# Where the sums of the modulation groups stand in a two-layer trunk kernel, and the order of its last norm

## The chip, the cores and the metric

The kernel runs on one core of a Trainium2 chip. The metric is the device time of one execution in microseconds (us). Before the change it is 2019.62 us, the median of 3 runs (2019.18 to 2021.65).

The core has a matrix engine (TensorE, PE, with its weight loads listed as PEld), a vector engine (VectorE, DVE), a scalar engine (ScalarE, ACT), GpSimd (POOL) and SyncE (SP), whose queue issues most DMA transfers. Each engine works through its own instructions in order.

## The reference

A trunk of two layers (T = 512 tokens, D = 1024, float32). Each layer has a mixer sub-layer and a feed-forward (FFN) sub-layer, and both are modulated by a vector c (adaLN):

```
m = silu(c) @ w_ada + b_ada          # six groups of 1024 values for each layer
h = rms_norm(x) * gain * (1 + scale) + shift          # groups 0 and 1 (mixer), 3 and 4 (FFN)
z = h @ w_in                          # inputs of three branches, and three gates
y_a = head_rms(scan_a(...)) * sigmoid(a_g)            # gated recurrence, both directions
y_b = head_group_norm(scan_b(...)) * silu(b_g)        # retention, both directions
y_c = head_rms(scan_c(...)) * silu(c_g)               # gated linear attention, both directions
mixed = sum over branches of sigmoid(gate) * (y @ w_p)
x = x + m[2] * (mixed @ w_out)                        # group 2
x = x + m[5] * ((silu(g) * u) @ w_ffn_out)            # g, u = h @ w_ffn_in; group 5
```

After the last layer comes a final RMS norm with a gain, which is the output.

## The kernel before

**Matrix products.** Every float32 product is three products of halves: an operand is split into a high part and the rest, and `three` (L278) adds hi·hi, lo·hi and hi·lo. Weights come in tiles of 128 x 4 x 256 (512 KB). `weight` (L259) takes a buffer `raw` (a pool of 3) and loads it on SP's queue; `parts` (L268) splits a part of the tile, high part by ACT (L274), rest by DVE (L275), into buffers of which there are four each. A tile has two splits, and its `raw` buffer is free once both are done. Names of tiles carry the layer, the matrix and the place: `L0fg6w40l` is layer 0's FFN matrix g, column block 6, rows from 4 on, half 0, the rest (l) of the split (h is the high part).

**The order of the work.** A scheduler sorts each engine's instructions by its own estimate of when they are due. `tc.high_priority` moves some ahead, `tc.issue_after` holds an instruction behind another in the schedule, and `in_order` (L103) ties a piece of the program to the order in which it is written. The boundary between two sub-layers is written with `in_order`; the last norm is not.

**The stages of a layer.** Input products and three branches with their scans; a tail of the mixer (the C branch's last levels `L0CQ`, `L0CK`, `L0Ct`, the gates `ga`, `gb`, `gc`, the products `mpa`, `mpb`, `mpc` and the gate products `mga`, `mgb`, `mgc`); `wo` (w_out); a boundary (`fz`, `fy`, `fx`: rest of w_out, norm, first products of the FFN); `fg` and `fu` (w_ffn_in); `fo` (w_ffn_out); the next boundary.

**Modulation groups.** Groups 0 and 1 of layer 0 are computed at the start, beside the first products. The other ten are background work: each is 16 pieces `wr` of 128 x 512 (256 KB, a pool of 2 buffers, loaded on SP's queue in program order, L204), and each piece is summed against `cact` (silu of c) by one DVE instruction (L210); the last piece of a group also finishes it (L214, L215). `bg_step` (L235) issues the load of the next piece and the sum of the piece loaded the step before. `weight` calls it `k.rate` times behind a tile's load, as long as the group is within `k.ahead`: twice a tile in the mixer's tail and w_out (`RATE`, L54, set at L1149), once a tile in the FFN (L1197). `bg_until` (L246) forces what is left of a group ahead of the place that needs it: group 2 before w_out, group 4 before the FFN's boundary, group 5 before `fo`, and the next layer's group 1 before its boundary.

**The start.** `first_products` (L533) works in eight rounds, one for each 128 rows of x. A round on DVE has two splits of weights, two small instructions, `x0t` (L600), the lower part of `h` (L603), which needs its high part from ACT (L602), and two sums `dot` (L565) for the next round.

**The end.** `last_norm` (L1061) makes the last products in two halves of the tokens, sums the squares (`finacc`), and for each half turns them into a factor for each token (PE `fin0tp`, DVE `fin0r`, POOL, DVE `fin0dg`, PE `fin0bc`), then makes eight outputs (L1078) and stores four of them with each transfer.

Of the kernel before, what the change touches and what calls it, by code (L numbers as in the profile page):

```python
# [50 lines left out]
LATE = (1, 1, 2)  # L51
LAG = 1
LAG1 = 1
RATE = 2  # L54

LEAF = (0, 1, 2, 4, 8, 16)

# [14 lines left out]
class Filler:  # L72
# [43 lines left out]
def trunk_kernel(ctx: ExitStack, tc: tile.TileContext, a, out):  # L116
# [11 lines left out]
    def duo(name, dt=F32, shape=(P, 2, 2, 512)):  # L128
        return sp.tile(list(shape), dt, tag="s", name=name)
# [14 lines left out]
    def xt(kk):  # L144
        return k.xd[kk // 4][:, kk % 4]
# [86 lines left out]
                st.enter_context(tc.issue_after(i.ins))  # L232
            yield

    def bg_step(upto=(DEPTH, 0)):  # L235
        if bg and bg[0][0] <= upto:
            _, (load, step) = bg.pop(0)
            with behind():
                if not k.loaded:
                    load()  # L240
                if bg:
                    bg[0][1][0]()
                k.loaded = True
                step()
# [14 lines left out]
    def weight(src, kn, cols, name):  # L259

        raw = wp.tile([P, 4, 256], F32, tag="raw", name=name)
        nc.sync.dma_start(raw[:, :kn, :cols], src.rearrange("(k p) n -> p k n", p=P))  # L262
        if k.ahead:
            for i in range(k.rate):
                bg_step(k.ahead)
        return raw

    def parts(raw, name):  # L268

        shape = list(raw.shape)  # L270
        hi = wp.tile(shape, F32R, tag="hi", name=name + "h", bufs=4)
        lo = wp.tile(shape, F32R, tag="lo", name=name + "l", bufs=4)
        with behind(), tc.high_priority(offset=k.prio):
            nc.scalar.copy(hi, raw)  # L274
            nc.vector.tensor_sub(lo, raw, hi.bitcast(F32))  # L275
# [257 lines left out]
    def first_products():  # L533
# [57 lines left out]
        def before(kk):  # L591

            hl = [parts(loads[kk][1][:, :3, i * P:(i + 1) * P], f"L0A0w{kk}{i}") for i in range(2)]
            m = mod[0][:, 0:2, kk]
            nc.vector.tensor_add(m, m, acol[:, 0:16].rearrange("p (g k) -> p g k", g=2)[:, :, kk])
            gm = gmul[0][:, 0, kk:kk + 1]
            nc.vector.scalar_tensor_tensor(gm, mod[0][:, 1, kk:kk + 1], 1.0, acol[:, R_N1 + kk:R_N1 + kk + 1],
                                           op0=ALU.add, op1=ALU.mult)
            t, sh = tmp(f"x0t{kk}"), mod[0][:, 0, kk:kk + 1]
            nc.vector.scalar_tensor_tensor(t, xt(kk), gm, bc, op0=ALU.mult, op1=ALU.mult)  # L600
            hi, lo = h[0][kk // 2][:, kk % 2], h[1][kk // 2][:, kk % 2]
            nc.scalar.activation(hi, t, AF.Identity, bias=sh)  # L602
            nc.vector.scalar_tensor_tensor(lo, t, sh, hi.bitcast(F32), op0=ALU.add, op1=ALU.subtract)  # L603
# [456 lines left out]

    def last_norm(block, add):  # L1061
        acc = squares("fin")
        for n in range(4):
            block(0, n)
        norm = half_norm(acc, 0, add, "fin0")
        for _ in range(7):
            bcs = [next(norm)]
        for n in range(4):
            block(1, n)
        norm = half_norm(acc, 1, add, "fin1")  # L1070
        with tc.high_priority(offset=EVAC):
            for _ in range(7):
                bc = next(norm)
        for hv, bc in enumerate(bcs + [bc]):
            od = duo(f"out{hv}", shape=(P, KD, T // 2))
            for kk in range(KD):
                gf = pcol[:, R_NF + kk:R_NF + kk + 1]
                nc.vector.scalar_tensor_tensor(od[:, kk], xt(kk)[:, half(hv)], gf, bc, op0=ALU.mult, op1=ALU.mult)  # L1078
                if kk % 4 == 3:
                    dst = out[(kk - 3) * P:(kk + 1) * P, half(hv)].rearrange("(j p) t -> p j t", p=P)  # L1080
                    nc.sync.dma_start(dst, od[:, kk - 3:kk + 1])


    for l in range(DEPTH):
# [44 lines left out]
        with tc.tile_pool(name=f"att{l}", bufs=2) as k.att:  # L1129
            halves = lambda t: [t[:, 0], t[:, 1]]  # L1130
            y = {"A": halves(claimed(f"L{l}Ay"))}
            lev, tail_a = run(branch_a(l, 0, z0), PACE[0])
            run(lev(), PACE[0])
            done_a = gain_done(l, "A", R_NA, y["A"])
            tail_b = both(branch_b(l, fill.get("zb")), tail_a(va, done_a), PACE[1])
            y["B"] = halves(claimed(f"L{l}By"))
            tail_b = tail_b(fill.get("vb"), gain_done(l, "B", R_NB, y["B"], True))
            lev, tail_a1 = both(branch_a(l, 1, fill.get("z1")), tail_b, PACE[2], 1)
            both(lev(), tail_b, PACE[2])
            lev, tail_c = both(branch_c(l, fill.get("zc")), tail_a1(va, done_a), PACE[3])  # L1140
# [12 lines left out]
        with tc.tile_pool(name=f"late{l}", bufs=1) as k.late:
# [35 lines left out]
            for n in range(KF // 2):  # L1189
                bk = gemmT(w, n * 256, 256, h, f"L{l}fg{n}") if n else first[0]  # L1190
                sg = []
                for i in range(2):
                    s = wk.tile([P, 512], F32, tag="t", name=f"L{l}fs{n}{i}", bufs=5)
                    nc.scalar.activation(s, bk[i], AF.Silu)
                    sg.append(s)
                bk = gemmT(w, DFF + n * 256, 256, h, f"L{l}fu{n}") if n else first[1]
                k.ahead, k.rate, k.prio = (l + 1, 1), 1, AHEAD  # L1197
                for i in range(2):
                    nc.vector.tensor_mul(sg[i], sg[i], bk[i])  # L1199
                    split(hd, 2 * n + i, sg[i])  # L1200
                if n:
                    k.behind = ()
# [74 lines left out]
```

## Time and profile before

| | us |
|---|---|
| median of 3 runs | 2019.62 (2019.18 to 2021.65) |
| profiled execution, its own time | 2018.08 |
| its span | 2016.3 |
| PE busy | 1926.5 (96%) |
| DVE busy | 1076.3 (53%) |
| ACT busy | 763.1 (38%) |
| POOL busy | 172.4 (9%) |
| DVE's sums of pieces (L210) | 111.6, 160 of them |
| DVE waiting for their transfers | 283.4, in 104 places |

The page's mean clock of PE is given as a share of full speed; it is 0.986 over the execution. A row of the waits names the waiting engine, its instruction and line, what ended the wait, and then the time in all, how often, and the longest. A row of a timeline has its start, its duration, engine, line and operation, what is written from what, and in brackets how long the engine stood idle before it and for what. A row of the table by stretches gives the stretch and its length, the busy time of each engine with its number of instructions, PE's granted clock, the busy share of the DMA engines, and GB/s. Idle time of an engine that is not the bound costs nothing by itself.

### The profile page before, as it was taken

To read this page: it belongs to the slowest core of one execution; us is meant where nothing else is said; L and a number is where in the kernel's file an instruction comes from. 1 tells how busy PE (TensorE), PEld (TensorE's weight loads), DVE (VectorE), ACT (ScalarE), POOL (GpSimd) and SP (SyncE) were. 2 spreads that over 40 slices of the span, in tenths; PEclk is the share of its full clock that TensorE was granted. 3 is DMA by queue.
4 is the path that set the end of the run, shared out by engine and by line. 5 is a ranking of instruction groups with operands and counts; after the bars stand their busy time and mean duration, and the time that the engine had idled before them with its cause. 6 is when DMAs were issued, how large, how long until landed. Compare 5 with 4: busy or idle time off the path is not lost. (4 is left out here: it accounts for less than half of the span.)

```text
span 2016.3 us, 32132 instructions
## 1 busy us (share of the span) xinstructions
PE 1926.5 (96%) x13288; PEld 1606.2 (80%) x13288; DVE 1076.3 (53%) x1917; ACT 763.1 (38%) x1273; POOL 172.4 (9%) x175
## 2 busy tenths in 40 slices
PE   5999999899999999999999999999999999999997
PEld 4898877777788887778889988777778888888886
DVE  6676586664436544443355756786553464433334
ACT  3544375432334332222345343653323353333321
POOL 0120111020111000000011101110111110000000
PEclk9999999999999999999999999999899999999998
DMA  9332223444323343433333322334543233333332
GB/s 337 94 106 77 64 77 90 150 149 151 115 94 110 120 141 126 141 125 126 115 120 91 106 76 57 94 97 125 167 156 96 94 121 126 115 95 94 99 94 69
DMA packets 196579, 231.91 MB, mean 115 GB/s; under 512 B 10640, under 2 KB 170640, under 8 KB 195408
## 3 DMA queue, kind: packets, MB, share of 16 engines
q1 hardware_dynamic: 194640, 224.77, 35.5%
q0 software_dynamic: 1504, 4.47, 0.8%
q8 instruction: 104, 1.70, 0.3%
q10 hardware_dynamic: 288, 0.61, 0.1%
q14 instruction: 43, 0.35, 0.1%
HBM read 221.43 MB, written 6.29 MB: 113 GB/s over the span
## 5 line engine op out<-in xcount | busy, mean ns | idle before, releaser
L210 DVE SCALAR_TENSOR_TENSOR wr<-wr,cact 128x512 f32<-128x512 f32 x160 | 111.6, 704 | 283.7 <-DMA wr<-w_ada 283.4
L334 ACT CAST L0hid<-L0fs 128x512 fp32r<-128x512 f32 x22 | 13.6, 621 | 84.5 <-DVE L0fs L1199 84.4
L348 POOL TENSOR_TENSOR L1h0r<-L1h0r,mhalf 128x2 f32<-128x2 f32 x1 | 1.1, 1082 | 358.2 <-DVE L1h0r L347 358.2
L348 POOL TENSOR_TENSOR fin0r<-fin0r,mhalf 128x2 f32<-128x2 f32 x1 | 0.7, 700 | 346.2 <-DVE fin0r L347 346.2
L565 DVE SCALAR_TENSOR_TENSOR fw<-fw,cact 128x1024 f32<-128x1024 f32 x16 | 19.0, 1219 | 0.0
L334 ACT CAST L1hid<-L1fs 128x512 fp32r<-128x512 f32 x22 | 13.7, 623 | 12.3 <-DVE L1fs L1199 11.4
L602 ACT ACTIVATE h<-x0t,mod 128x512 fp32r<-128x512 f32 x8 | 5.8, 722 | 31.9 <-DVE x0t L600 31.8
L1175 POOL TENSOR_TENSOR L0ma<-L0ma,L0sgb 128x512 f32<-128x512 f32 x6 | 9.8, 1638 | 90.6 <-DVE L0sgb L1174 90.6
L1175 POOL TENSOR_TENSOR L1ma<-L1ma,L1sgb 128x512 f32<-128x512 f32 x6 | 9.8, 1638 | 90.4 <-DVE L1sgb L1174 90.4
L1175 POOL TENSOR_TENSOR L1ma<-L1ma,L1sgc 128x512 f32<-128x512 f32 x8 | 12.7, 1599 | 52.0 <-DVE L1sgc L1174 52.0
L1175 POOL TENSOR_TENSOR L0ma<-L0ma,L0sgc 128x512 f32<-128x512 f32 x8 | 12.8, 1599 | 51.1 <-DVE L0sgc L1174 51.1
L577 PE MATMUL ssp<-ones,x0acc 128*128 128x1 f32 x8 | 1.9, 354 | 15.0 <-DVE x0acc L574 15.0
L335 DVE TENSOR_TENSOR L0hid<-L0fs,L0hid 128x512 fp32r<-128x512 f32 x22 | 15.1, 692 | 1.9
L335 DVE TENSOR_TENSOR L1hid<-L1fs,L1hid 128x512 fp32r<-128x512 f32 x22 | 15.2, 693 | 0.8
L686 DVE TENSOR_TENSOR L0AK<-L0AK,L0AG 128x1024 f32<-128x1024 f32 x12 | 14.6, 1216 | 0.7 <-POOL L0AG L678 0.7
L686 DVE TENSOR_TENSOR L1AK<-L1AK,L1AG 128x1024 f32<-128x1024 f32 x12 | 14.6, 1215 | 0.7 <-POOL L1AG L678 0.7
L678 POOL TENSOR_TENSOR L0AqT<-L0AG 128x1024 f32<-128x1024 f32 x2 | 8.0, 4018 | 78.6 <-DVE L0AG L868 78.6
L684 DVE TENSOR_TENSOR L0AQ<-L0AQ,L0AG 128x1024 f32<-128x1024 f32 x12 | 14.6, 1214 | 0.0
L684 DVE TENSOR_TENSOR L1AQ<-L1AQ,L1AG 128x1024 f32<-128x1024 f32 x12 | 14.6, 1213 | 0.0
L577 PEld LDWEIGHTS ssp<-ones,x0acc 128*128 128x128 f32 x8 | 1.8, 327 | 15.0 <-DVE x0acc L574 15.0
L210 DVE DVE_READ_ACCUMULATOR wr<-wr,cact 128x1 f32 x160 | 13.1, 82 | 0.0
L1032 ACT ACT_TABLE_LOAD x10 | 12.8, 1283 | 0.2
(5602 smaller groups left out, 6827.4 us busy)
## 6 DMA issues: line engine op xcount, KB each, us to landing
wr<-w_ada SPq DMA_DIRECT2D x160, 256.0 KB, 4.1
fw<-w_ada SPq DMA_DIRECT2D x16, 512.0 KB, 9.8
L0A0w<-w_in SPq DMA_DIRECT2D x8, 384.0 KB, 8.8
L0fo0w<-w_ffn_out SPq DMA_DIRECT2D x5, 512.0 KB, 3.5
L0fo1w<-w_ffn_out SPq DMA_DIRECT2D x5, 512.0 KB, 3.6
L0fo2w<-w_ffn_out SPq DMA_DIRECT2D x5, 512.0 KB, 3.4
L1hzw<-w_ffn_out SPq DMA_DIRECT2D x5, 512.0 KB, 3.4
L1fo0w<-w_ffn_out SPq DMA_DIRECT2D x5, 512.0 KB, 3.5
```

The source lines that it names most:

```text
L210: nc.vector.scalar_tensor_tensor(t, t, 1.0, cact[:, hlf * 512:hlf * 512 + 512], op0=ALU.mult, op1=ALU.mult, accum_out=st["sum"][:, hlf, j: ...
L334: nc.scalar.copy(h, src)
L335: return nc.vector.tensor_sub(dst[1][i // 2][:, i % 2], src, h.bitcast(F32))
L348: nc.gpsimd.tensor_tensor(r, r, mhalf[:, :w], op=ALU.pow)
L565: nc.vector.scalar_tensor_tensor(t, t, 1.0, cact, op0=ALU.mult, op1=ALU.mult, accum_out=mod[0][:, g, kk:kk + 1])
L577: nc.tensor.matmul(ps[:, c:c + 1], acc[:, c * P:(c + 1) * P], ones[:, :1], start=True, stop=True)
L602: nc.scalar.activation(hi, t, AF.Identity, bias=sh)
L678: nc.gpsimd.tensor_mul(tots[2 * s], t[:, :, :, 0], t[:, :, :, 1])
L684: nc.vector.tensor_mul(q, q, crossed(t, s, 1, d - 1, True))
L686: nc.vector.tensor_mul(kk, kk, crossed(t, s, d + 1, -d - 1, True))
L1032: nc.scalar.activation(z[:, i], z[:, i], func)
L1175: nc.gpsimd.tensor_add(acc[i], acc[i], sg[i])
```

## The change

- `bg_step` is parted. `bg_load` issues the load of one piece, at most two being begun; `bg_sum` issues a sum. `weight` calls `bg_load` once for each tile, in the mixer's tail too (`RATE` is gone), and notes in `k.due` how many sums are due. `parts` issues such a sum behind its own DVE split (`issue_after` on that instruction).
- In the mixer `k.ahead` is set earlier, ahead of the C branch's tail. In the FFN it reaches to group 2 of the next layer, one group further than before.
- In `first_products` one of the two `dot` sums stands between ACT's high part and DVE's lower part of `h`.
- `last_norm` is written in order, its outputs are spread over it, and a store takes two outputs in place of four.

```diff
@@
+    def bg_load(upto=(DEPTH, 0)):
+        if bg and bg[0][0] <= upto and len(k.begun) < 2:
+            tag, (load, step) = bg.pop(0)
             with behind():
+                load()
+            k.begun.append((tag, step))
+    def bg_sum(after=None):
+        with behind():
+            if after is None:
+                k.begun.pop(0)[1]()
+            else:
+                with tc.issue_after(after.ins):
+                    k.begun.pop(0)[1]()
     def bg_until(l, g):
-        while any(tag <= (l, g) for tag, _ in bg):
-            bg_step()
+        while any(tag <= (l, g) for tag, _ in k.begun + bg):
+            bg_load()
+            if len(k.begun) == 2 or not bg:
+                bg_sum()
+        k.due = 0
@@ weight
         if k.ahead:
-            for i in range(k.rate):
-                bg_step(k.ahead)
+            k.due = len(k.begun)
+            bg_load(k.ahead)
@@ parts
-            nc.vector.tensor_sub(lo, raw, hi.bitcast(F32))
+            last = nc.vector.tensor_sub(lo, raw, hi.bitcast(F32))
+        if k.due:
+            k.due -= 1
+            bg_sum(last)
@@ first_products
             nc.scalar.activation(hi, t, AF.Identity, bias=sh)
+            if kk + 1 < KD:
+                dot(kk + 1, 1)
             nc.vector.scalar_tensor_tensor(lo, t, sh, hi.bitcast(F32), op0=ALU.add, op1=ALU.subtract)
             if kk + 1 < KD:
-                dot(kk + 1, 1)
                 dot(kk + 1, 0)
@@ last_norm
-        for n in range(4):
-            block(0, n)
...
+        with in_order(tc):
+            for n in range(4):
+                block(0, n)
+            norm = half_norm(acc, 0, add, "fin0")
+            for _ in range(3):
+                next(norm)
+            block(1, 0)
+            block(1, 1)
+            for _ in range(3):
+                next(norm)
+            block(1, 2)
+            bcs.append(next(norm))
+            block(1, 3)
+            outputs(0, 0, 2)
+            norm = half_norm(acc, 1, add, "fin1")
+            for _ in range(5):
+                next(norm)
+            outputs(0, 2, 4)
+            next(norm)
+            bcs.append(next(norm))
+            outputs(0, 4, 8)
+            outputs(1, 0, 8)
@@ the layers
+            k.ahead = (l, 4)
             run(tail_c(fill.get("vc"), gain_done(l, "C", R_NC, y["C"])), PACE[5])
-        k.ahead, k.rate = (l, 4), RATE
...
-                k.ahead, k.rate, k.prio = (l + 1, 1), 1, AHEAD
+                k.ahead, k.prio = (l + 1, 2), AHEAD
```

How it moves instructions is shown at three places. First, DVE in the tail of layer 0's mixer, around the last level of the C branch; `wr` rows are the sums of pieces (group, block, half). Before:

```order
L275 TENSOR_TENSOR L0mpa0w00l<-L0mpa0w_4305,L0mpa0w00h 128x512
L214 TENSOR_TENSOR mod_93<-ms_2_4068 128x8
L215 TENSOR_TENSOR mod_93<-mod_93,cols 128x8
L275 TENSOR_TENSOR L0mpa0w01l<-L0mpa0w_4305,L0mpa0w01h 128x512
L275 TENSOR_TENSOR L0mpb0w00l<-L0mpb0w_4353,L0mpb0w00h 128x512
L210 SCALAR_TENSOR_TENSOR wr_3_0_1_4443,ms_3_4445<-wr_3_0_1_4443,cact 128x512
L684 TENSOR_TENSOR L0CQ<-L0CQ,L0CG 128x2x8x64
L686 TENSOR_TENSOR L0CK<-L0CK,L0CG 128x2x8x64
L210 SCALAR_TENSOR_TENSOR wr_3_1_0_4447,ms_3_4445<-wr_3_1_0_4447,cact 128x512
L275 TENSOR_TENSOR L0mpb0w01l<-L0mpb0w_4353,L0mpb0w01h 128x512
L210 SCALAR_TENSOR_TENSOR wr_3_1_1_4490,ms_3_4445<-wr_3_1_1_4490,cact 128x512
L210 SCALAR_TENSOR_TENSOR wr_3_2_0_4493,ms_3_4445<-wr_3_2_0_4493,cact 128x512
```

The same place with the change:

```order
L283 TENSOR_TENSOR L0mpa0w00l<-L0mpa0w_4296,L0mpa0w00h 128x512
L209 SCALAR_TENSOR_TENSOR wr_2_3_1_4230,ms_2_3877<-wr_2_3_1_4230,cact 128x512
L283 TENSOR_TENSOR L0mpa0w01l<-L0mpa0w_4296,L0mpa0w01h 128x512
L283 TENSOR_TENSOR L0mpb0w00l<-L0mpb0w_4341,L0mpb0w00h 128x512
L209 SCALAR_TENSOR_TENSOR wr_2_4_0_4298,ms_2_3877<-wr_2_4_0_4298,cact 128x512
L696 TENSOR_TENSOR L0CQ<-L0CQ,L0CG 128x2x8x64
L698 TENSOR_TENSOR L0CK<-L0CK,L0CG 128x2x8x64
L283 TENSOR_TENSOR L0mpb0w01l<-L0mpb0w_4341,L0mpb0w01h 128x512
L283 TENSOR_TENSOR L0mgc0w00l<-L0mgc0w_4384,L0mgc0w00h 128x512
L209 SCALAR_TENSOR_TENSOR wr_2_4_1_4343,ms_2_3877<-wr_2_4_1_4343,cact 128x512
```

There is one sum for each weight tile in place of two, each right behind the tile's first split, and the pieces are at group 2 where they were at group 3 before.

Second, SP's queue in layer 0's FFN, the loads (`fg`, `fu`: weight tiles) around column block 6. Before:

```order
L262 DMA L0fg6w_7132<-w_ffn_in 128x4x256
L204 DMA wr_0_2_1_7134<-w_ada 128x512
L262 DMA L0fg6w_7169<-w_ffn_in 128x4x256
L204 DMA wr_0_3_0_7171<-w_ada 128x512
L262 DMA L0fu6w_7212<-w_ffn_in 128x4x256
L204 DMA wr_0_3_1_7214<-w_ada 128x512
```

With the change:

```order
L269 DMA L0fg6w_7132<-w_ffn_in 128x4x256
L203 DMA wr_0_2_0_7089<-w_ada 128x512
L269 DMA L0fg6w_7169<-w_ffn_in 128x4x256
L203 DMA wr_0_2_1_7134<-w_ada 128x512
L269 DMA L0fu6w_7212<-w_ffn_in 128x4x256
L203 DMA wr_0_3_0_7171<-w_ada 128x512
```

On DVE, the sum behind the first split of the first fg6 tile is that of wr_0_3_1 before (its load stands behind fu6's tile, two tiles further on) and that of wr_0_2_0 with the change (its load stands behind the fg6 tile itself).

Third, DVE at the end of layer 0's w_out, with the change; before, no sum stands here:

```order
L283 TENSOR_TENSOR L0wo2w00l<-L0wo2w_5796,L0wo2w00h 128x512
L209 SCALAR_TENSOR_TENSOR wr_4_5_1_5757,ms_4_5354<-wr_4_5_1_5757,cact 128x512
L283 TENSOR_TENSOR L0wo2w01l<-L0wo2w_5796,L0wo2w01h 128x512
L209 SCALAR_TENSOR_TENSOR wr_4_6_1_5835,ms_4_5354<-wr_4_6_1_5835,cact 128x512
L1210 SCALAR_TENSOR_TENSOR L0x_4885<-L0wo1b_5716,mod_93,L0x_4885 128x512
L283 TENSOR_TENSOR L0wo2w40l<-L0wo2w_5833,L0wo2w40h 128x512
L209 SCALAR_TENSOR_TENSOR wr_4_6_0_5798,ms_4_5354<-wr_4_6_0_5798,cact 128x512
L414 TENSOR_TENSOR L0facc<-L0facc,L0fsq_5889 128x512
L209 SCALAR_TENSOR_TENSOR wr_4_7_0_5872,ms_4_5354<-wr_4_7_0_5872,cact 128x512
L1210 SCALAR_TENSOR_TENSOR L0x_4885<-L0wo1b_5717,mod_93,L0x_4885 128x512
L283 TENSOR_TENSOR L0wo2w41l<-L0wo2w_5833,L0wo2w41h 128x512
L209 SCALAR_TENSOR_TENSOR wr_4_7_1_5875,ms_4_5354<-wr_4_7_1_5875,cact 128x512
```

The last five sums of group 4 now stand among the splits of w_out's last tiles; in layer 1 the group ends among the mixer's gate products, as both layers' do before.

More of the change, by code (lines that the diff above doesn't have):

```diff
@@ L53 @@
 LAG1 = 1
-RATE = 2
 LEAF = (0, 1, 2, 4, 8, 16)
@@ L233, in behind @@
             yield
-    def bg_step(upto=(DEPTH, 0)):
-        if bg and bg[0][0] <= upto:
-            _, (load, step) = bg.pop(0)
+    def bg_load(upto=(DEPTH, 0)):
+        if bg and bg[0][0] <= upto and len(k.begun) < 2:
+            tag, (load, step) = bg.pop(0)
             with behind():
[L239 to L244, printed above, removed]
-    def bg_until(l, g):
-        while any(tag <= (l, g) for tag, _ in bg):
-            bg_step()
-    k.ahead, k.rate, k.prio, k.behind, k.loaded = None, 1, 0, (), False
+                load()
[7 more added lines that the diff above has]
+                    k.begun.pop(0)[1]()
+    def bg_until(l, g):
+        while any(tag <= (l, g) for tag, _ in k.begun + bg):
[3 more added lines that the diff above has]
+        k.due = 0
+    k.ahead, k.prio, k.behind, k.begun, k.due = None, 0, (), [], 0
     def log_exp_table(after):
@@ L1062, in last_norm, with outputs @@
         acc = squares("fin")
-        for n in range(4):
-            block(0, n)
[L1065 to L1076, printed above, removed]
-                gf = pcol[:, R_NF + kk:R_NF + kk + 1]
[L1078 to L1081, printed above, removed]
+        ods = [duo(f"out{hv}", shape=(P, KD, T // 2)) for hv in range(2)]
+        bcs = []
+        def outputs(hv, k0, k1):
+            od = ods[hv]
+            for kk in range(k0, k1):
+                gf = pcol[:, R_NF + kk:R_NF + kk + 1]
+                nc.vector.scalar_tensor_tensor(od[:, kk], xt(kk)[:, half(hv)], gf, bcs[hv], op0=ALU.mult, op1=ALU.mult)
+                if kk % 2:
+                    dst = out[(kk - 1) * P:(kk + 1) * P, half(hv)].rearrange("(j p) t -> p j t", p=P)
+                    nc.sync.dma_start(dst, od[:, kk - 1:kk + 1])
+        with in_order(tc):
[20 more added lines that the diff above has]
+            outputs(1, 0, 8)
     for l in range(DEPTH):
```

## Prediction

> **What bounds the kernel now.** I read the page's busy line and chain first, then the waits of each engine, then a table of stretches, and last the timelines of the stretches in which TensorE (PE) waits.
>
> ```profile
> PE 1926.5 (96%) x13288; PEld 1606.2 (80%) x13288; DVE 1076.3 (53%) x1917; ACT 763.1 (38%) x1273; POOL 172.4 (9%) x175
> ...
> DMA wr<-w_ada 5%; DVE wr L210 1%; PE L1fo2b L279 1%; PE L1fo1b L279 1%; PE L1fo0b L281 0%; PE L1fo0b L279 0%; PE L1fo2b L281 0%; PE L1fo1b L281 0%; PE L1fo1b L280 0%; PE L1fo0b L280 0%; PE L1fo2b L280 0%; SPq L262 0%; PE finza L279 0%; PE finza L281 0%; PE finza L280 0%
> ```
>
> PE bounds the span: it is busy for 1926.5 of 2016.3 us, so every microsecond to be won is idle time of PE (89.8 us) or time in which it runs slowly. The one thing that stands in the chain beside PE is a transfer, a modulation piece `wr`, with 5% (about 100 us). Next, the waits: who waits for these pieces, and where PE waits.
>
> ```profile
> DVE wr L210 <- DMA wr<-w_ada: 283.4, 104, 5.1
> ```
> ```profile
> PE L0A0b L279 <- ACT h L602: 9.0, 7, 1.9
> PE fin1tp L419 <- DVE finacc L415: 3.7, 1, 3.7
> PE L0Ct L834 <- DVE L0Cn L831: 3.3, 1, 3.3
> ...
> PE L0Cl L713 <- DVE L0CQ L684: 2.8, 3, 1.5
> ...
> PE L1Cl L713 <- DVE L1CQ L684: 2.8, 3, 1.4
> PE L1mga2b L280 <- DVE L1mga2w41l L275: 2.6, 1, 2.6
> ...
> PE L1Ct L834 <- ACT L1yc L334: 2.3, 1, 2.3
> ...
> PE L1Ct L834 <- DVE L1Cn L831: 1.3, 1, 1.3
> ```
>
> VectorE (DVE) stands still for 283.4 us, in 104 places, until a piece lands. DVE is busy for only 53%, so this costs nothing by itself; it costs where the instruction queued behind the piece's sum is one that PE needs. The PE rows show such instructions: the weight tiles' splits (`...w41l`, L275) and a scan operand (`CQ`). The table by stretches says where.
>
> ```profile
> 300.00:525.00 225.00, 206.06 (x1892) 168.29 (x1891) 139.20 (x279) 88.22 (x150) 23.17 (x23) 0.96 0.44 138
> ...
> 1300.00:1525.00 225.00, 206.51 (x1880) 168.12 (x1879) 137.58 (x277) 87.17 (x148) 24.42 (x23) 0.95 0.42 134
> 1700.00:1900.00 200.00, 200.00 (x883) 165.53 (x882) 77.81 (x122) 64.69 (x108) 0.00 (x0) 1.00 0.33 104
> ```
>
> The columns are length, busy time of PE, weight loads, DVE, ACT, POOL, then PE's granted clock. In the two mixer tails (300 to 525, 1300 to 1525) PE is idle for 18.9 and 18.5 us and its clock is 0.96 and 0.95. In layer 1's FFN (1700 to 1900), where few pieces are left, it is busy throughout at 1.00.
>
> **Part 1, a sum behind a split, one transfer per tile: the mixer tails.** How one piece stops PE:
>
> ```profile
> 387.35 0.69 DVE L210 SCALAR_TENSOR_TENSOR wr<-wr,cact 128x512 f32<-128x512 f32 x1 [4.01 <-DMA wr<-w_ada]
> ...
> 389.11 1.22 DVE L686 TENSOR_TENSOR L0CK<-L0CK,L0CG 128x1024 f32<-128x1024 f32 x1
> ```
> ```profile
> 390.47 1.51 PE L758 MATMUL L0Ckt<-ident,L0CK 128*128 128x128 f32 x6 [2.84 <-DVE L0CK L686]
> ```
> ```profile
> 390.00:395.00 5.00, 4.53 (x16) 4.08 (x17) 1.54 (x4) 1.38 (x3) 0.00 (x0) 0.50 0.46 135
> ...
> 435.00:440.00 5.00, 5.00 (x18) 4.02 (x17) 2.77 (x6) 0.62 (x1) 0.30 (x1) 0.76 0.85 359
> ```
>
> DVE waits 4.01 us for the piece; CQ (1.22 us, like CK) and CK stand behind its sum and are done that much later; PE waits 2.84 us and then runs at a clock of 0.50, and in a later case at 0.76 while busy for all 5 us. So a wait costs its length and a slow stretch behind it. The two tails together lose 18.9 + 18.5 = 37.4 us of idle, and at most 0.04 x 225 + 0.05 x 225 = 20.3 us of clock: 57.7 us (upper end, since clock lost during an idle is counted twice). The Trainium skill, "TensorE: Matmul & The Clock Gate", Part 1, says the clock falls after an idle window of about 3.4 us. Here 2.84 us were enough, so the trace does not bear that out as a threshold on the wait's length; by that rule waits that are all under 3.4 us would cost no clock, the 20.3 us would have another cause and stay, and the sum would come out near 1975.
>
> What the change does here: before, two loads per tile are issued, and the sum's turn on DVE comes right behind the split that released the weight buffer for which the queue was standing. In the new order SP takes the weight tile, then one piece, and the sum of that piece stands behind the first split of the very weight tile that was loaded with it. The next piece waits on SP for the sum two pieces earlier. Between a piece's issue and its sum lie about two weight tiles. A tile holds PE for about 5.5 us (fo0 rows below: one tile of 24 products from 1879.3 to 1884.8), so some 11 us stand against the landing:
>
> ```profile
> wr<-w_ada SPq DMA_DIRECT2D x160, 256.0 KB, 4.1
> ```
>
> So the sums should find their data. Each still takes 0.69 + 0.08 us of DVE, half as many per tile as before, in a stretch where DVE is busy for 62% (139.20 of 225). What stays is the chain that has nothing to do with pieces: the C branch's normalisation into Ct (3.3 + 2.3 + 1.3 us) and the levels' CQ into Cl (2.8 + 2.8): 12.5 us, with some 1.5 us of clock, 14 in all. Gain taken: 57.7 - 14 = **43.7 us**; lower end, half of the idle alone, 18.7 us.
>
> **Part 2, the same in layer 0's FFN.** The two layers do the same work there, so the price can be read directly.
>
> ```profile
> L279 PE MATMUL L0fzb<-L0m,L0fzw00h x8: 278/280/282, 630.0 to 636.7; 128*128 128x256 f32 x8
> L279 PE MATMUL L1fzb<-L1m,L1fzw00h x8: 278/280/283, 1622.5 to 1629.2; 128*128 128x256 f32 x8
> L279 PE MATMUL L0fo0b<-L0hid,L0fo0w00h x4: 394/394/398, 899.4 to 901.5; 128*128 128x512 f32 x4
> L279 PE MATMUL L1fo0b<-L1hid,L1fo0w00h x4: 394/394/398, 1879.3 to 1881.3; 128*128 128x512 f32 x4
> L279 PE MATMUL L1fo0b<-L1hid,L1fo0w40h x4: 394/396/397, 1884.8 to 1886.9; 128*128 128x512 f32 x4
> ```
>
> From the first product of the boundary to the first of the FFN's second matrix: layer 0 takes 899.4 - 630.0 = 269.4 us, layer 1 1879.3 - 1622.5 = 256.8. The difference, 12.6 us, is what the pieces cost. The mechanism:
>
> ```profile
> 776.23 0.38 SPq L262 DMA_DIRECT2D L0fu6w<-w_ffn_in  x1
> 776.66 0.50 SPq L204 DMA_DIRECT2D wr<-w_ada  x1
> ```
> ```profile
> 780.78 0.69 DVE L210 SCALAR_TENSOR_TENSOR wr<-wr,cact 128x512 f32<-128x512 f32 x1 [3.97 <-DMA wr<-w_ada]
> ```
>
> SP can load fu6's tile only when a split releases a buffer, at 776.2; the piece behind it goes out at 776.66 and its sum is one split further on DVE: the whole landing is waited for, once per tile. In the new order that piece goes out two tiles ahead of its sum. I keep 0.6 us for DVE's extra work: gain **12.0 us**, lower end 6.
>
> **Part 3, layer 0's w_out, where the pieces run out of tiles (a loss).** At one piece a tile, group 4 of layer 0 is not finished when it is wanted, and the last sums are forced. DVE's new order has the split wo2w01l, then the sum of wr_4_6_1; wo2w40l, then the sums of wr_4_6_0 and wr_4_7_0; wo2w41l, then wr_4_7_1. The load of 4_6_1 needs the buffer of 4_5_1, summed one split earlier, and 4_7_0 that of 4_6_0, summed just ahead: two waits of the old kind. On SP the last three pieces stand in front of the fyw tiles. Now:
>
> ```profile
> 619.85 0.69 DVE L275 TENSOR_TENSOR L0wo2w41l<-L0wo2w,L0wo2w41h 128x512 fp32r<-128x512 f32 x1
> ...
> 624.73 1.29 DVE L448 TENSOR_TENSOR L0fy<-L0fyw,L0fy 128x512 fp32r<-128x512 f32 x2 [1.44 <-ACT L0fy L447]
> ...
> 632.63 0.68 DVE L275 TENSOR_TENSOR L0fzw41l<-L0fzw,L0fzw41h 128x512 fp32r<-128x512 f32 x1
> ```
> ```profile
> 620.57 5.85 SPq L262 DMA_DIRECT2D L0fyw<-w_ffn_in  x2
> ```
> ```profile
> L279 PE MATMUL L0wo2b<-L0m,L0wo2w41h x4: 394/396/397, 627.2 to 629.3; 128*128 128x512 f32 x4
> ```
> ```profile
> L279 PE MATMUL L0fzb<-L0m,L0fzw41h x8: 278/282/365, 634.2 to 642.5; 128*128 128x256 f32 x8
> ```
>
> Two waits of 4.1 us, less the work between (a split and an add, about 1.5 us, ahead of the first), and four sums of 0.77 move wo2w41l from 619.85 by about 6.5 us to 626.3; PE wants it at 627.2, so it just holds. The fyw load, released by that split, moves from 620.57 to about 627, its split from 624.73 to 631.5, and fzw41l from 632.63 to about 637.5, while PE wants it at 634.2: PE would wait about 3.5 us, partly with a slow clock behind it. I take **4 us lost**; ends 0 (the slack holds) and 8 (both fy splits late, and the clock). Layer 1 starts its group early enough that none is forced.
>
> **Part 4, the start.**
>
> ```profile
> 28.14 0.75 DVE L600 SCALAR_TENSOR_TENSOR x0t<-x,gmul,x0bc 128x512 f32<-128x512 f32 x1
> 29.68 0.75 DVE L603 SCALAR_TENSOR_TENSOR h<-x0t,mod,h 128x512 fp32r<-128x512 f32 x1 [0.79 <-ACT h L602]
> 30.35 1.22 DVE L565 SCALAR_TENSOR_TENSOR fw<-fw,cact 128x1024 f32<-128x1024 f32 x1
> ...
> 33.97 0.75 DVE L600 SCALAR_TENSOR_TENSOR x0t<-x,gmul,x0bc 128x512 f32<-128x512 f32 x1
> ```
>
> A round takes 33.97 - 28.14 = 5.83 us on DVE and PE waits for it (9.0 us, 7 times). DVE waits 0.79 us for ACT in each; the change puts one of the two 1.22-us sums there. The lower half of h then comes 0.43 us later in its round, but the round shrinks by 0.79: 7 x 0.79 = **5.5 us** gained. Lower end 0 (PE then waits for the later lower half), upper 6.3 with one split moved behind the last x0t.
>
> **Part 5, the end.**
>
> ```profile
> 2001.51 3.22 DVE L1078 SCALAR_TENSOR_TENSOR out<-L1x,cols,fin0bc 128x256 f32<-128x256 f32 x8
> 2004.65 0.42 DVE L415 TENSOR_TENSOR finacc<-finacc,fin1sq 128x256 f32<-128x256 f32 x1
> ```
>
> The second half's sum of squares stands behind eight outputs (3.22 us, and PE's fin1tp waits 3.7). In the new order only two outputs of 0.40 stand ahead of it, so about 2.4 us are freed; the last store holds half the bytes, estimated 0.7 us less. Against this PE makes fin0bc ahead of its last block, about 0.9 us. Net **2 us** gained, ends 0 and 3.5.
>
> **The sum.** 2018.08 (the profiled execution) - 43.7 - 12.0 + 4 - 5.5 - 2 = 1958.9 us. The median shown is 2019.62, 1.5 above the profiled execution, so **1960 us** is predicted for the median.
>
> **Rivals.** (a) The scan's own chain sets the tails: the pieces' waits go, but PE meets the same C-branch dependencies a little earlier, and only 18.7 us come back. 1960 + 25 = 1985. For it: a third of the tails' idle already names Cn, CQ and yc. Against: those rows are themselves late by pieces, as CK at 389.11 is. (b) Nothing stays: FFN 12.6, tails 57.7, no loss at w_out: 2018.1 - 57.7 - 12.6 - 5.5 - 2 + 1.5 = 1942. (c) The idle goes and the slow clock stays: of the 43.7 us the clock's share 20.3/57.7, 15.4 us, is not won: 1975. Against it: the stretch without waits (1700 to 1900) has 1.00. (The Trainium skill's rule quoted in part 1 would speak for it.) (d) The other side: SP's queue. Now each weight tile's load stands behind a piece that waits for a sum, which waits behind a split. If splits run late on DVE, the piece is issued late, its sum waits for landing, the next split is later still, and the loop settles at the old wait, but with all 160 pieces in it. At today's price, 70.3 us (57.7 + 12.6) over the 104 waiting sums, 0.68 us each, 160 cost 108 us: 2019.6 + 108 - 70.3 + 4 - 7.5 = 2054. It decides from (70.3 + 7.5 - 4) / 160 = 0.46 us per piece. Against it: a tile's split and its piece's sum are two tiles apart, so a split must be over 6 us late (11 less 4.1, less a sum) for the loop to begin, and DVE has 47% of its time to catch up. (e) It doesn't do what it says: the waits vanish on DVE but none of PE's idle was theirs, leaving parts 3 to 5: 2019.6 + 4 - 7.5 = 2016, within what can't be told apart.
>
> **How the numbers follow.** Forecast 0.60, (a) 0.16, (b) 0.11, (c) 0.05, (d) 0.05, (e) 0.03. For the range I go to (b) at the low end with the end terms at their best, 1938, and at the high end past (a) with a start that gives nothing, 1985 + 5 = 1990; outside lie (d), (e) and a little of (a). A measurement of this kernel tells about 0.2% (4 us) from no change. Faster by more: forecast, (a), (b), (c), 0.92; same: (e), 0.03; slower: (d), 0.05.
>
> **What the profile after would show.** Right: DVE's wait for `wr` falls from 283.4 to under 30 us, most of it at w_out; layer 0 takes at most 258 us from its fzb to its fo0; the tails' granted clock is 0.98 or more and PE's idle in each below 8 us; rounds at the start of 5.0 us; fin1tp waits under 1.5 us. Part 3 shows as PE waiting for fzw01l, fy or fzw41l in layer 0 alone. Wrong: DVE's waits for `wr` stay above 100 us (d), or vanish while Ct, Cl and Ckt keep PE as idle as now (a), or the tails' clock stays at 0.96 with little idle (c).

## The result and the profile after

The changed kernel takes 1951.88 us (median of 4 runs, 1951.0 to 1955.11) against 2019.4 us before; the ratio is 0.967 with a 95% interval of 0.965 to 0.968. The profiled execution's span falls from 2016.3 to 1949.6 us.

The page of the changed kernel, its busy line and its chain of what ended last:

```profile
PE 1901.3 (98%) x13288; PEld 1598.1 (82%) x13288; DVE 1086.7 (56%) x1917; ACT 766.4 (39%) x1273; POOL 172.0 (9%) x175
...
PE L1fo2b L290 1%; PE L1fo1b L290 1%; PE L1fo0b L290 1%; PE L1fo0b L292 1%; PE L1fo2b L292 1%; PE L1fo1b L292 1%; PE L1fo1b L291 1%; PE L1fo0b L291 1%; PE L1fo2b L291 1%; PE L1Cl L725 0%; PE finza L290 0%; PE finza L292 0%; PE finza L291 0%; PE L1A1l L725 0%; PE L1A0l L725 0%
...
L209 DVE SCALAR_TENSOR_TENSOR wr<-wr,cact 128x512 f32<-128x512 f32 x160 | 121.9, 762 | 2.4 <-DMA wr<-w_ada 2.4
...
wr<-w_ada SPq DMA_DIRECT2D x160, 256.0 KB, 2.7
```

No transfer stands in the chain any more. DVE's 160 sums take 121.9 us and wait 2.4 us in all, where they waited 283.4. PE's busy time fell too, by 25 us for the same 13288 products; its mean granted clock over the execution is 0.996 where it was 0.986. The same table by stretches, with the two tails of the mixer at their new places and the stretch of layer 0's boundary:

```profile
300.00:500.00 200.00, 196.43 (x1893) 163.22 (x1892) 124.81 (x232) 87.74 (x150) 23.00 (x22) 1.00 0.42 124
...
605.00:615.00 10.00, 8.14 (x52) 7.77 (x52) 6.07 (x13) 4.19 (x9) 1.09 (x1) 0.83 0.43 131
...
1260.00:1460.00 200.00, 196.43 (x1879) 162.82 (x1878) 127.14 (x236) 86.53 (x147) 24.66 (x23) 0.99 0.41 125
```

In each tail PE now does as many products within 200 us (1893 and 1879) as it did within 225 (1892 and 1880), idles for 3.6 us instead of 18.9 and 18.5, and its granted clock is 1.00 and 0.99 instead of 0.96 and 0.95. What PE still waits for:

```profile
PE ssp L588 <- DVE x0acc L585: 15.5, 1, 15.5
...
PE L0mpc0b L290 <- ACT L0sgc L1194: 2.8, 1, 2.8
PE L1mpc0b L290 <- ACT L1sgc L1194: 2.8, 1, 2.8
PE L0A0b L290 <- ACT h L613: 1.9, 1, 1.9
...
PE fin1tp L430 <- DVE finacc L426: 1.6, 1, 1.6
...
PE L0fzb L291 <- DVE L0fzw41l L283: 1.2, 1, 1.2
...
PE L0fzb L290 <- ACT L0fzw41h L282: 0.7, 1, 0.7
```

In the tails the waits for CK, CQ, Cn and the splits are gone. New or longer are the wait for the bank of `mpc0` (2.8 us in each layer, where layer 1 had 0.8 and layer 0 none) and that for the boundary's `fzw41` in layer 0 (1.9 us). To see where the 66.7 us went, I took the start of the first product of a stage in each kernel (one row each, such as these two for layer 0's boundary and the FFN's second matrix in the changed kernel):

```profile
L290 PE MATMUL L0fzb<-L0m,L0fzw00h x8: 278/279/415, 600.6 to 611.2; 128*128 128x256 f32 x8
...
L290 PE MATMUL L0fo0b<-L0hid,L0fo0w00h x4: 394/394/397, 861.3 to 863.4; 128*128 128x512 f32 x4
```

and subtracted the lengths of the stages of before. Each number is a kernel's stage length less that of before, in us, from one profile each:

| stage, by its first and last product | change | pieces alone | start alone | norm alone | no tie | rate one | one buffer | no pieces | earlier begin |
|---|---|---|---|---|---|---|---|---|---|
| start, to L0Av0 | -5.5 | 0.2 | -6.3 | 0.1 | -6.5 | 2.1 | -6.5 | -6.5 | -6.2 |
| layer 0, L0Av0 to L0A1l | 1.0 | 1.0 | 0.6 | 0.6 | 0.5 | -0.1 | 0.9 | 0.9 | 1.0 |
| layer 0's tail, to L0wo0 | -24.9 | -23.2 | -0.8 | 0.3 | 2.7 | 0.1 | -23.4 | -20.7 | -24.9 |
| w_out, to L0fzb | 0.0 | 0.0 | 0.0 | 0.0 | 5.3 | 7.2 | 0.1 | 0.0 | 0.0 |
| boundary, to L0fg1 | 3.9 | 3.9 | 0.0 | 0.0 | 1.9 | 4.9 | 1.1 | 0.0 | 0.0 |
| FFN, to L0fo0 | -12.6 | -12.6 | 0.3 | -1.8 | 2.9 | 3.4 | -12.6 | -12.6 | -12.6 |
| fo and layer 1, to L1A1l | -1.2 | 0.6 | 2.8 | 2.6 | 3.7 | 2.5 | 0.0 | 0.4 | 0.1 |
| layer 1's tail, to L1wo0 | -24.8 | -24.7 | -2.4 | -3.5 | 2.1 | -2.3 | -24.9 | -23.3 | -26.1 |
| layer 1, to finzb | 0.0 | 0.0 | 0.0 | 0.0 | 0.0 | 10.4 | 0.0 | 0.0 | -0.1 |
| end | -2.6 | 0.0 | -0.1 | -2.9 | -2.6 | 0.2 | -2.7 | -2.9 | -2.6 |
| span | -66.7 | -54.8 | -5.9 | -4.6 | 10.0 | 28.4 | -68.0 | -64.7 | -71.4 |

Three rows also move in the two kernels that edit only the start or only the norm: "fo and layer 1" by 2.6 and 2.8 us, layer 1's tail by -3.5 and -2.4, the FFN by up to -1.8. So in these rows 4 us from one profile prove nothing; the first two together move by under 1 us there. The rows w_out and boundary don't move at all in these two kernels, so what they show elsewhere is the edit's.

### The profile page after: what moved, and what is told of

The parts are those of the page before. It is cut to its first block, busy times and chain, and to the rows that moved or that the text cites. A ratio compares the mean times of both kernels' runs of the same rounds, so it can differ in the third digit from the quotient of the medians.

```text
span 1949.6 us, 32291 instructions
## 1 busy us (share of the span) xinstructions
PE 1901.3 (98%) x13288; PEld 1598.1 (82%) x13288; DVE 1086.7 (56%) x1917; ACT 766.4 (39%) x1273; POOL 172.0 (9%) x175
## 5 line engine op out<-in xcount | busy, mean ns | idle before, releaser
L209 DVE SCALAR_TENSOR_TENSOR wr<-wr,cact 128x512 f32<-128x512 f32 x160 | 121.9, 762 | 2.4 <-DMA wr<-w_ada 2.4
L613 ACT ACTIVATE h<-x0t,mod 128x512 fp32r<-128x512 f32 x8 | 5.8, 725 | 24.7 <-DVE x0t L611 24.7
```

Source lines behind the costliest of these rows:

```text
L209: nc.vector.scalar_tensor_tensor(t, t, 1.0, cact[:, hlf * 512:hlf * 512 + 512], op0=ALU.mult, op1=ALU.mult, accum_out=st["sum"][:, hlf, j: ...
```

## The experiments

**The three parts apart.** The change has three independent edits. The first kernel keeps the edit on the pieces and takes back the other two.

```diff
 (the changed kernel, with first_products and last_norm as before)
```

> The change to the pieces alone, the start and the last norm as before. Theory (the parts are independent and add up): all of the change but the start's 5.6 us and the end's 2.6 us, so about 1960 us, ratio 0.971; DVE's wait for wr under 10 us. Rival (the parts hide one another, for instance the last norm's order matters only where the FFN runs ahead): 1952 or above 1965.

Measured 1962.42 us (1960.73 to 1963.91), ratio 0.971 (0.970 to 0.973): near the sum that was expected, 1960. DVE's wait for `wr` is 2.5 us in all.

```diff
 (the kernel before, with this alone)
             nc.scalar.activation(hi, t, AF.Identity, bias=sh)
+            if kk + 1 < KD:
+                dot(kk + 1, 1)
             nc.vector.scalar_tensor_tensor(lo, t, sh, hi.bitcast(F32), op0=ALU.add, op1=ALU.subtract)
             if kk + 1 < KD:
-                dot(kk + 1, 1)
                 dot(kk + 1, 0)
```

> The kernel before with only the dot sum moved in the start. Theory (each round shrinks by the 0.79 us that DVE waited for ACT): L0Av0's first product 5.6 us earlier and the whole about 2014 us, ratio 0.9972. Rival (the first level of branch A then waits for DVE, as it did for 1.1 us in the profile after): the first product is 5.6 us earlier but only 4.5 us arrive at the end, 2015, ratio 0.9978.

Measured 2011.01 us (2009.14 to 2012.43), ratio 0.995 (0.994 to 0.997). The profile has 6.3 us in the start and 5.9 in all; the times have 8.2, with an interval that reaches down to 6.5, so the 5.6 us of the theory are a little too few, and what the rest is stays open. Nothing of it is given back in branch A beyond what that stage gives in kernels without this edit (0.6 us here; 1.0 and 0.6 with the pieces or the norm alone), so the rival falls.

```diff
 (the kernel before, with the change's last_norm alone)
```

> The kernel before with only the new last norm. Theory (six outputs fewer ahead of the second half's sum of squares, a smaller last store, against a later last product): 2.6 us less, 2016.8, ratio 0.9987. Rival (the later products cost what is won): 2019.4, ratio 1.000.

Measured 2017.27 us (2013.47 to 2022.69, 12 runs), ratio 0.9987 (0.9976 to 0.9997). The interval leaves out no change (the rival) only just; the stage "end" shows 2.9 us, and nothing else there was edited. The three parts together make 54.8 + 5.9 + 2.9 = 63.6 us by their profiles (of the norm's only its own stage), and 56.8 + 8.2 + 1.9 = 66.9 by their times, against 66.7 and 67.5 for the change: they add up, to some 3 us.

**What in the first part wins: the tie to the split, or one sum for a tile?** The next kernel undoes the tie only.

```diff
         if k.due:
             k.due -= 1
-            bg_sum(last)
+            bg_sum()
```

> The changed kernel, but the sum isn't tied behind the split: still one piece for each tile, two begun. Theory (what counts is the distance on the queues between a piece's load and its sum's turn, and the tie gives it): DVE's wait for wr is back above 150 us, the FFN of layer 0 takes 269 us again in place of 257, the tails lose about half of what they lost before (half as many sums), together about 1952 + 12.6 + 25 = 1990. Rival (one sum for each tile in place of two is what won): 1952 to 1957, the FFN stays at 257.

Measured 2030.57 us (2028.04 to 2032.29), ratio 1.005 (1.003 to 1.007): not the 1990 of the theory, and slower than the kernel before. The waits of this kernel, DVE's for the pieces and one of PE's, and DVE's sums in the first tail (300 to 525), first this kernel's and then, of before, the same group:

```profile
DVE wr L209 <- DMA wr<-w_ada: 433.5, 145, 5.6
```
```profile
PE L0A1kt L770 <- DVE L0A1u0M L807: 4.2, 1, 4.2
```
```profile
L209 DVE SCALAR_TENSOR_TENSOR wr<-wr,cact 128x512 f32<-128x512 f32 x29 | 20.6, 709 | 74.2 <-DMA wr<-w_ada 74.2
```
```profile
L210 DVE SCALAR_TENSOR_TENSOR wr<-wr,cact 128x512 f32<-128x512 f32 x48 | 33.8, 712 | 55.9 <-DMA wr<-w_ada 55.8
```

In the FFN, a piece's load on SP and its sum on DVE, without the tie and then with it (the changed kernel); both loads go out behind a tile of `fg6`:

```profile
774.74 0.49 SPq L203 DMA_DIRECT2D wr<-w_ada  x1
...
778.63 0.69 DVE L209 SCALAR_TENSOR_TENSOR wr<-wr,cact 128x512 f32<-128x512 f32 x1 [3.76 <-DMA wr<-w_ada]
```
```profile
735.70 0.34 SPq L203 DMA_DIRECT2D wr<-w_ada  x1
...
745.82 0.69 DVE L209 SCALAR_TENSOR_TENSOR wr<-wr,cact 128x512 f32<-128x512 f32 x1
```

Without the tie the scheduler sets the sum, here, two tiles earlier on DVE than the tie does, among the splits of `fu5`, as it did before: 3.9 us lie between load and sum in place of 10.1, and DVE stands still for the landing. 145 of the 160 sums wait. This kernel has the gains of the start and the end too (-6.5 and -2.6 us in the table), so its pieces cost some 19 us more than those of the kernel before. And the number of sums is not what counts: with 29 sums in place of 48 the stretch waits longer (2.6 us each in place of 1.2), because before, the two sums of a tile shared one wait. My half was wrong for that reason: a wait comes with each tile, not with each sum. The same shows from the other side:

```diff
-RATE = 2
+RATE = 1
```

> The kernel before with one piece for each tile in the mixer's tail in place of two, nothing else. Theory (distance, not number): every sum still stands one split behind its load's place and waits; the tails lose half as often, about 25 us less than before, the FFN keeps its 12.6 us, and forced sums ahead of the FFN's boundary in both layers cost 4 to 8 us: about 2000. Rival (the number of sums is what counts): the tails win all their 50 us, about 1970.

Measured 2047.92 us (2045.01 to 2050.28), ratio 1.014 (1.012 to 1.016): neither the 2000 of the theory nor the rival's 1970. That nearly every sum waits holds; what this costs was put far too low.

```profile
DVE wr L210 <- DMA wr<-w_ada: 421.0, 139, 5.4
```

One piece for each tile in the old scheme wins nothing in the tails (0.1 and -2.3 us) and leaves pieces over that are forced at w_out and at the boundary, in both layers: 12 us in layer 0 and 10 in layer 1. So the slower rate that the change brings with it is by itself a loss of 28 us; with the tie its cost is the 3.9 us at layer 0's boundary. The old rate of two pieces for each tile was not run with the tie, so what the tie alone would win there is not shown.

**How much distance is needed.** With one buffer a piece's load has to wait for the last piece's sum, so it goes out one tile ahead of its own sum, not two.

```diff
-            t = st[j, hlf] = wp.tile([P, 512], F32, tag="ada", name=f"wr{l}_{g}_{j}_{hlf}", bufs=2)
+            t = st[j, hlf] = wp.tile([P, 512], F32, tag="ada", name=f"wr{l}_{g}_{j}_{hlf}", bufs=1)
```

> The changed kernel with one buffer for the pieces in place of two: the load of a piece waits for the sum of the last one, so the distance between load and sum is one tile (5.5 us) in place of two. Theory (the distance has to exceed the landing, 2.7 to 4.1 us, and a sum, 0.77 us, and no more): within 4 us of the changed kernel, 1952 to 1956, DVE's wait for wr under 40 us. Rival (two tiles are needed): FFN of layer 0 back at 265 us or more and the whole above 1970.

Measured 1949.47 us (1948.73 to 1950.24), ratio 0.965 (0.964 to 0.967). The sums of all pieces in this kernel, and one piece's load on SP and its sum on DVE in the FFN:

```profile
L209 DVE SCALAR_TENSOR_TENSOR wr<-wr,cact 128x512 f32<-128x512 f32 x160 | 121.4, 759 | 4.8 <-DMA wr<-w_ada 4.8
```
```profile
744.19 0.33 SPq L203 DMA_DIRECT2D wr<-w_ada  x1
```
```profile
748.91 0.69 DVE L209 SCALAR_TENSOR_TENSOR wr<-wr,cact 128x512 f32<-128x512 f32 x1
```

A piece issued at 744.19, behind the sum before it (743.47 to 744.2), is summed at 748.91, 4.7 us later and without a wait: one tile (5.5 us) is enough. DVE waits 4.8 us in all, and the FFN is the same to a tenth. The second buffer bought nothing: every run with one buffer is faster than the fastest of the changed kernel (1951.0), and layer 0's boundary loses 1.1 us where that loses 3.9.

**The floor.** All background pieces are left out: neither loads nor sums; groups 2 to 5 of layer 0 and all of layer 1 are a constant.

```diff
         def load(j, hlf):
+            return
...
-            nc.vector.scalar_tensor_tensor(t, t, 1.0, cact[...], ..., accum_out=st["sum"][:, hlf, j:j + 1])
+            if j == KD - 1 and hlf:
+                nc.vector.memset(st["sum"], 0.01)
```

> The changed kernel without the 160 background pieces: neither loads nor sums, the modulation groups 2 to 5 of layer 0 and all of layer 1 are filled with a constant (this part of the computation is left out). It gives the floor. Theory (the pieces now cost only the forced ones at layer 0's w_out): 3.9 us less than the changed kernel, 1948, and PE's waits for L0mpc0 and L1mpc0 (2.8 us each) are still there. Rival (their DVE time of 123 us still delays the scans): under 1942, and the waits for mpc0 go.

Measured 1952.1 us (1951.02 to 1953.33), ratio 0.9665 (0.965 to 0.968): no faster than the changed kernel, so that the 1948 of the theory and the rival's 1942 are both missed. Its boundary is 3.9 us shorter, but its tails are 4.2 and 1.5 us longer (the second within what that row moves by itself). The waits in this kernel show why; its order differs, and PE meets the C branch's norm in place of `mpc0`'s bank:

```profile
PE L1Ct L843 <- DVE L1Cn L840: 4.1, 2, 3.2
PE L0Ct L843 <- DVE L0Cn L840: 4.1, 2, 3.2
```

So 40 MB of pieces and their 122 us of DVE cost the changed kernel no time on balance. But this is not a strict floor: without the pieces the scheduler takes another order, and in it PE waits 4.1 us for Cn in each layer though no piece stands in the way. This wait then belongs to the C branch's own chain, and the order decides whether PE meets it.

**A version without forced sums.** The mixer's background work begins one step earlier.

```diff
+            k.ahead = (l, 4)
             run(lev(), PACE[4])
-            k.ahead = (l, 4)
             run(tail_c(fill.get("vc"), gain_done(l, "C", R_NC, y["C"])), PACE[5])
```

> The changed kernel with the background work of the mixer's tail begun one step earlier, ahead of the C branch's levels, so that no sum is forced at layer 0's w_out. Theory (the forced sums cost 3.9 us there and a begun piece costs nothing elsewhere): L0fzb starts and ends without a wait, 1948 us. Rival (sums among the C branch's levels delay CQ and CK by 0.77 us each and PE waits for Cl): 1952 or more.

Measured 1947.79 us (1946.7 to 1948.57), ratio 0.964 (0.963 to 0.966). No run of it is as slow as the fastest of the changed kernel (1951.0). In its profile the boundary is as long as before (0.0 where the change has 3.9), DVE waits for no piece at all (its row of sums, below), and all sums of layer 0's group 4 are done before w_out's last tiles are split (at 577 us, the first of these splits at 581). The rival's cost is there as well, 2.0 us of PE waiting for `L1Cl` on CQ, but layer 1's tail as a whole is no longer for it (-26.1). The theory's 1948 is met, and the kernel is faster than the changed one.

```profile
L209 DVE SCALAR_TENSOR_TENSOR wr<-wr,cact 128x512 f32<-128x512 f32 x160 | 120.9, 755 | 0.0
```
```profile
PE L1Cl L725 <- DVE L1CQ L696: 2.0, 1, 2.0
```

Two more were built on it:

```diff
 (the kernel with the earlier begin, and bufs=1 for the pieces)
```

> The changed kernel with the earlier begin and with one buffer for the pieces. Theory (one buffer won 2.4 us only at layer 0's w_out, where the earlier begin leaves nothing to win): as the earlier begin alone, 1947 to 1949. Rival (one buffer lets weight tiles leave SP earlier everywhere): 1945 or less.

Measured 1950.4 us (1949.59 to 1952.49), ratio 0.965 (0.964 to 0.967). It is not faster, so the rival falls, and a little slower than the theory's 1947 to 1949. By its profile, against the earlier begin alone, it loses 1.7 us in layer 0's tail, 1.6 in layer 1's and 2.6 in "fo and layer 1", and DVE waits 5.8 us for pieces. Whether one buffer costs something here or the last two are the variation of those rows stays open.

```diff
     def gated(zs, func, y, name):
...
+        if name.endswith("yc"):
+            with tc.issue_after(act.ins):
+                nc.scalar.preload_act_table_set("sigmoid_and_others")
```

> The changed kernel with the earlier begin, and with ACT's table for the sigmoid loaded right behind the last silu of the C gate, long ahead of mgc0's sigmoid. Theory (PE's 2.8 us for L0mpc0 hold a table load of 1.28 us on ACT between mgc0's last product and its sigmoid, which frees the bank): that wait falls to 1.5 us in layer 0, 1.3 us less in all, 1946.5. Rival (the activations ahead of the sigmoid set the wait, the table load only fills it): L0mpc0 still waits 2.5 us or more, 1948.

Measured 1948.45 us (1948.16 to 1951.72), ratio 0.964 (0.963 to 0.966). The waits of this kernel:

```profile
PE L1mpc0b L290 <- ACT L1sgc L1197: 1.3, 1, 1.3
PE L0mpc0b L290 <- ACT L0sgc L1197: 1.3, 1, 1.3
```

The theory of the wait holds: 2.77 us became 1.34 in layer 0, about the table load's 1.28 us less, and layer 0's tail is 1.2 us shorter than with the earlier begin alone. But in layer 1, where that kernel had no wait for `mpc0`, one appears, and the whole isn't faster: the 1946.5 of the theory is missed. Why layer 1 is sorted differently was not looked into; the time as a whole tells no difference.

## Why the prediction was right

Forecast 1960, measured 1951.9: right in direction, within the range and by the mechanism that was named, 8 us too high. By its terms:

| step | predicted | measured (profile) |
|---|---|---|
| part 1, the tails | -43.7 | -24.9 - 24.8 = -49.7 |
| part 2, the FFN | -12.0 | -12.6 |
| part 3, layer 0's w_out | +4 | +3.9 |
| part 4, the start | -5.5 | -5.5 |
| part 5, the end | -2 | -2.6 |
| not foreseen (layer 0 before its tail, fo and layer 1's first stages) | 0 | -0.2 |
| sum | -59.2 | -66.7 |

**Part 1: the term that was mis-sized is "what stays", 14 us.** I left the waits for Cn and CQ to the scan's own chain, because their rows name no piece. In the profile after there is none of them, and what does stay is 3.6 us of idle in each tail and some 2 us of clock, 9 us in place of 14. CQ was late by pieces: the kernel without pieces has no wait for it, and 2.0 us of it come back where sums stand among the levels again (the earlier begin). For Cn my reading was not wrong, since PE waits for it in the kernel without pieces as well; that it doesn't in the changed kernel is a matter of the new order, which I did not foresee. The upper end, idle plus clock, 57.7 us, was a good measure: taking off what is there now (3.6 + 3.6 us idle, and 0.01 x 200 = 2 us of clock) leaves 48.5 against 49.7 measured. The 2.8 us for `mpc0`'s bank in each layer I did not foresee either; the experiment with the sigmoid's table shows 1.4 us of layer 0's to go with a table load on ACT. Layer 1's idle before also held 3.0 us (`L1Cl`, put down to "issue", for which the profile shows no cause) that are gone after; why stays open.

**Part 2** was read off a twin: layer 1 did the same work without pieces, and layer 0's FFN now has that length (the stage is 12.6 us shorter, all of the difference). I kept 0.6 us for DVE's extra work; it costs nothing. My mark of at most 258 us from fzb to fo0 failed (861.3 - 600.6 = 260.7), since it took in the boundary's 3.9.

**Part 3: the size was right, the way there only in part, and so the size is in part luck.** I expected two waits of a whole landing, 4.1 us, wo2w41l and fyw's load over 6 us late, and PE waiting for about 3.5 us. On DVE, the two waits in the changed kernel, and what came late behind them; and on SP the three pieces ahead of fyw:

```profile
586.07 0.69 DVE L209 SCALAR_TENSOR_TENSOR wr<-wr,cact 128x512 f32<-128x512 f32 x1 [0.47 <-DMA wr<-w_ada]
...
591.47 0.69 DVE L209 SCALAR_TENSOR_TENSOR wr<-wr,cact 128x512 f32<-128x512 f32 x1 [1.90 <-DMA wr<-w_ada]
...
598.69 1.29 DVE L459 TENSOR_TENSOR L0fy<-L0fyw,L0fy 128x512 fp32r<-128x512 f32 x2 [3.09 <-ACT L0fy L458]
...
606.52 0.68 DVE L283 TENSOR_TENSOR L0fzw41l<-L0fzw,L0fzw41h 128x512 fp32r<-128x512 f32 x1
```
```profile
586.79 5.72 SPq L203 DMA_DIRECT2D wr<-w_ada  x3
593.45 0.38 SPq L269 DMA_DIRECT2D L0fyw<-w_ffn_in  x1
```

The waits are 0.47 and 1.90 us, 2.4 together. fyw leaves 2.3 us late (593.45 against 620.57 less the 29.4 us by which this stage now starts earlier), fy's split is 3.4 late and fzw41l 3.3 (606.52 against 632.63 - 29.4). PE then waits 1.9 us and runs at 0.83 for 10 us, at most 1.7 more: 3.6 of the 3.9. Half the wait that I expected and a larger share of slow clock made the 4 us. That the forced sums are the cause is shown by the earlier begin: without them the stage is as before.

**Part 4.** In the changed kernel x0t's eight rows, and then the row of the timeline in which h waited for ACT before:

```profile
L611 DVE SCALAR_TENSOR_TENSOR x0t<-x,gmul,x0bc x8: 746/747/750, 22.8 to 58.0; 128x512 f32<-128x512 f32 x8
```
```profile
28.39 1.22 DVE L576 SCALAR_TENSOR_TENSOR fw<-fw,cact 128x1024 f32<-128x1024 f32 x1
29.53 0.75 DVE L616 SCALAR_TENSOR_TENSOR h<-x0t,mod,h 128x512 fp32r<-128x512 f32 x1
```

Seven rounds take 35.2 us, 5.03 each, as 5.83 less 0.79 gives, and no wait stands ahead of h. That the stage gains just 5.5 us is in part luck: the first x0t comes 0.5 us later than before in this profile (22.8, before 22.3), and one of the seven rounds takes 5.6 us where the others take 4.9. The start alone, with all rounds at 4.9, gains 6.3. The later lower half of h costs PE little: 0.3 us in each of four rounds.

**Part 5.** Only two outputs stand ahead of the second half's sum now (rows of the changed kernel), and fin1tp waits 1.6 us in place of 3.7 (my mark was under 1.5):

```profile
1936.08 0.87 DVE L1082 SCALAR_TENSOR_TENSOR out<-L1x,cols,fin0bc 128x256 f32<-128x256 f32 x2 [0.80 <-PE fin0bc L440]
...
1938.47 0.42 DVE L426 TENSOR_TENSOR finacc<-finacc,fin1sq 128x256 f32<-128x256 f32 x1 [0.15 <-ACT fin1sq L423]
```

How much of the 2.6 us is the order and how much the smaller stores was not tried apart, so the 0.7 us that I gave to the stores is shown by no run.

**The rivals.** (a), the scan's chain setting the same stalls, falls by the tails. (b), nothing stays, was no nearer than the forecast: 1942 is 10 us too low as 1960 is 8 too high, its 57.7 us for the tails are 8 too many as my 43.7 are 6 too few, and w_out has the loss that it leaves out. (c), the slow clock staying, falls: 1.00 and 0.99. (d), the loop in which every sum waits, does not occur here. A kernel in which nearly every sum waits exists, the one without the tie (145 waits, 2030.6 us), but it gets there another way: not by splits that run late on DVE, as I wrote, but by where the scheduler puts the sum. (e) falls: PE's idle went with DVE's waits.

## What to carry to other kernels

A background transfer is hidden only if its consumer's turn on its engine is farther behind its issue than its landing, and both places are set by queues: look up which buffer the queue's next load waits for, and put the consumer far enough behind that release (here one tile, 5.5 us, against a landing of 2.7 us). The scheduler's own order undid this here, so tie the consumer to an instruction of the main stream; thinning out the background work without the tie made it worse. Where one layer of a network does the same work without the background, the difference of its stages is a good estimate of the price (12.6 us, of which the change won 12.6).

## What the hardware showed that was not expected

A piece lands in 2.7 us (median) where it took 4.1. Before, it left 0.4 us behind a weight tile of 512 KB (776.23 and 776.66); now it leaves 3.3 us behind one, as these rows of SP's queue in the changed kernel's FFN show:

```profile
737.82 0.37 SPq L269 DMA_DIRECT2D L0fg6w<-w_ffn_in  x1
741.14 0.34 SPq L203 DMA_DIRECT2D wr<-w_ada  x1
743.21 0.37 SPq L269 DMA_DIRECT2D L0fu6w<-w_ffn_in  x1
```

The other kernels agree: with the pieces 0.4 us behind a weight tile, as without the tie (774.30 and 774.74), the median is 3.9 us; with the tie and one buffer, 3.3 us behind (740.86 and 744.19), it is 2.6. That the two transfers share the DMA engines is argued from this, not shown apart.

The clock does not answer to the length of a single wait alone. Before, 2.84 us of idle (the row at 390.47) were followed by a clock of 0.50. After, PE waits 2.76 us ahead of `mpc0` in both layers: in layer 0 the clock stays at 1.00, in layer 1 it falls to 0.71 in the stretch behind the wait. The waits, and the stretches of 5 us around them, in the changed kernel:

```profile
414.55 0.50 PE L290 MATMUL L0mpc0b<-L0yc,L0mpc0w00h 128*128 128x512 f32 x1 [2.76 <-ACT L0sgc L1194]
```
```profile
410.00:415.00 5.00, 2.24 (x12) 1.66 (x11) 3.82 (x7) 3.81 (x7) 1.31 (x2) 1.00 0.19 35
415.00:420.00 5.00, 5.00 (x26) 4.14 (x25) 1.82 (x3) 1.72 (x3) 2.68 (x2) 1.00 1.05 426
```
```profile
1370.72 0.50 PE L290 MATMUL L1mpc0b<-L1yc,L1mpc0w00h 128*128 128x512 f32 x1 [2.76 <-ACT L1sgc L1194]
```
```profile
1370.00:1375.00 5.00, 4.28 (x13) 3.30 (x14) 2.29 (x4) 1.65 (x4) 2.98 (x2) 0.71 0.99 353
```

The traces of before and after also hold a list of clock changes, from some 30 us into the span on. In both the granted clock is either 1.00 or 0.50, and each stretch at 0.50, but for the one at the kernel's end, lasts 3.41 us or two or three times that. Before there are eight of them, 44.4 us together; after there are two, 6.8 us. Half of the difference, 18.8 us, is the most that the clock gave of the 66.7.

The Trainium skill, "TensorE: Matmul & The Clock Gate", Part 1, has a free-running window of about 3.4 us. The lengths of the slow stretches agree with it. Taken as a bare length of a wait, the rule fits the wait in layer 0 after the change and neither of the other two; something else, such as where a wait lies in the window or what PE did just ahead of it, must decide, and no run here settles it.
